# A hybrid encoder block in float32: where the second norm puts its squares, when its transposes run, and where the first values stand

## The chip, the core and the metric

The kernel runs on one core of one Trainium2 chip. Its engines work at the same time, each through its own list of instructions in order: TensorE (PE in the profile; PEld is its loading of weights), VectorE (DVE), ScalarE (ACT), GpSimd (POOL) and SyncE (SP), which here only issues loads and stores. They wait for one another by semaphores. The metric is the device time of one execution in microseconds (us), the median of several runs.

## The reference

One layer of a hybrid block on x of 1024 tokens by 1024 channels, all in float32:

```python
xn = rmsnorm(x, norm1_g[layer])
u = xn @ w_in[layer].astype(f32)
...
o_sb = stick_breaking_attention(split_heads(q_sb, SB_HEADS), split_heads(k_sb, SB_HEADS),
                                split_heads(v_sb, SB_HEADS))
...
h = x.astype(f32) + merged @ w_out[layer].astype(f32)
hn = rmsnorm(h, norm2_g[layer])
a = jnp.square(jax.nn.relu(hn @ w_ff1[layer].astype(f32)))
h = h + a @ w_ff2[layer].astype(f32)
...
return rmsnorm(h, final_g).astype(x.dtype)
```

Between the two norms lie eight heads of stick-breaking attention, four heads of a gated linear recurrence (HGRN2) and a gated merge of the two branches; the change does not touch them.

## The kernel before

**Precision.** Each float32 matrix is kept as a high and a low part: `hi_copy` (line 132, ACT) rounds to the high part, `lo_sub` (line 135, DVE) subtracts it. `three` makes a product of three matmuls, high by high, high by low and low by high. So every operand costs one ACT and one DVE instruction before PE can use it.

**Buffers.** `slot` gives one of 40 tiles of 128 by 1024, `bank` one of eight PSUM banks of 128 by 512, and the pool `wts` has two buffers each for raw, high and low weights. When a buffer is asked for and none is free, the instruction that writes it waits for the last reader of the one that is given back. Tokens are handled in eight blocks of 128 (`tb`), the first four of which are one half. Loads on SP keep their order (`load`, line 128); at most eight are open at once, so the ninth waits for the first to land.

**Order.** The text fixes the order of PE with `open_block` and `pe`; `Stream` holds jobs (projections of `w_in` and `w_out`) as generators, which `advance` and `finish` step. `after` adds an ordering edge without data. A scheduler then orders each engine's list.

**The start** (lines 150 to 200 and 1400 to 1412). SP loads x blocks 0 to 3, then six small parameter rows (`prow`), the first query/key weight (`wqk0`), x blocks 4 to 7 and the first value weight (`wv0`, two pieces). PE transposes `prow` (bank `ppar`), DVE copies it to `prm`, and a few tiny instructions make the lower bounds of the recurrence. `norm1_half` squares each block on ACT with a running sum (`token_rstd`, line 215), POOL makes the inverse root, DVE scales the block in place (line 512). `norm_transpose` transposes a half on PE, 32 transposes into eight banks `xnt`; ACT and DVE evacuate each bank into the high and low parts `xnh`, `xnl` (lines 255, 256). The first job (`first_job`) is the query/key projection of head 0: `proj_half` runs 24 matmuls of 512 columns into `pjqk` for half 0; then the second half of x is normed and transposed, 24 matmuls for half 1 follow, and then `token_steps` makes the values, 24 matmuls of 256 columns into `pjv` for each of the eight token blocks. The epilogue of `pjqk` writes `KS`, `QH`, `QL`; that of `pjv` writes `V`. After this the attention scores begin (`z`).

**The second norm** (lines 1005 to 1015 and 1476 to 1530). The last column half of `w_out` (`pw`) runs over the eight token blocks, 24 matmuls each; DVE adds each into `h` (line 1039). `norm2_token` squares the block on ACT into a slot of its own (`n_scr`), takes a further slot `hn` for the scaled block (line 1010) and stores `h` for later. `Quads` holds the transposed result in four quarters of the channels and tokens, `raw[q, kp]`. `fill(pr)` transposes two of the blocks, 16 transposes into four banks `hnt`, and ACT copies each bank in two parts into `hnq` (line 293): first quarters q 0 and q 1 of a bank, then the next bank. `plain` splits the q 0 parts of forms 1 and 2 into `sqh`, `sql`; `sums` builds the sums and differences of Strassen's scheme (line 313, `sq` and `hnq`) and `sum_form(i)` splits those into the forms 3 to 7. The first two column pairs of the up projection (`first`, class `UpPair`) then use them: `w1` multiplies form 1 and copies the bank `pW` to `p` (line 1143), `w2` adds form 2, `x6` and `x7` go to bank `pX`, `y5` to `pY`. `w1` and `w2` run in two halves of 256 columns, since columns 256 to 511 need the blocks 4 to 7. `sum_split` prepares the weights `t1h`, `t1l`, `t0h`, `t0l`.

In the driver, fills 0, 1 and 2 stand at blocks 4, 5 and 7, each after that block's `pw` matmuls and ahead of its squares; `plain` and `sums` follow them. Fill 3 comes after both pairs' `w1` and `w2` on columns 0 to 255.

Of the kernel before, what the change touches and what calls it, by code (L numbers as in the profile page):

```python
# [19 lines left out]
P = 128  # L20
# [19 lines left out]
def kernel(  # L40
# [89 lines left out]

    def hi_copy(dst, src):
        nc.scalar.copy(dst, src)  # L132

    def lo_sub(dst, src, hi):
        nc.vector.tensor_tensor(out=dst, in0=src, in1=hi.bitcast(F32), op=ALU.subtract)  # L135

    def hi_lo(h, l, src):
        hi_copy(h, src)
        lo_sub(l, src, h)
# [22 lines left out]
    for src, n in (  # L162
# [9 lines left out]

    pt = bank("ppar")
# [9 lines left out]
    nc.vector.tensor_tensor(  # L183
        out=lmx, in0=prm[:, LB0 : LB0 + 4], in1=prm[:, LB1 : LB1 + 4], op=ALU.max
    )
    for j in range(2):
        nc.vector.tensor_tensor(
            out=le[:, 4 * j : 4 * j + 4],
            in0=prm[:, LB0 + 4 * j : LB0 + 4 * j + 4],
            in1=lmx,  # L190
            op=ALU.subtract,
        )
    nc.scalar.activation(le, le, AF.Exp)
    nc.vector.tensor_tensor(out=lmx, in0=le[:, 0:4], in1=le[:, 4:8], op=ALU.add)
    nc.vector.reciprocal(lmx, lmx)
    mul(lb, le[:, 0:4], lmx)
    nc.vector.tensor_scalar(
        out=oml, in0=lb, scalar1=-1.0, scalar2=1.0, op0=ALU.mult, op1=ALU.add
    )
# [10 lines left out]
    last_evac = [None]  # L210

    def token_rstd(src, name):
        scr = slot(f"{name}_scr")
        ssq = small.tile([P, 1], F32, tag="ssq1", name=f"{name}_ss", bufs=4)
        after(nc.scalar.activation(scr, src, AF.Square, accum_out=ssq), last_evac[0])
        return inv_rms(ssq, 1, 1.0 / D, name)
# [49 lines left out]
    class Quads:  # L266
# [10 lines left out]
        def fill(self, pr, src, name):  # L277

            for kp in range(KT // 2):
# [12 lines left out]
                for q in range(2):  # L292
                    last_evac[0] = nc.scalar.copy(
                        self.part(self.raw[q, kp], pr, 1),
                        pb[:, q * 256 : (q + 1) * 256].rearrange("p (k t) -> p k t", k=2),
                    )

        def split(self, i, kp, src, pr=0, n=4):
            if (i, kp) not in self.hl:
                self.hl[i, kp] = tuple(slot(f"sq{n_}{i}{kp}", F32R) for n_ in "hl")  # L300
            h, l = (self.part(t, pr, n) for t in self.hl[i, kp])
            hi_lo(h, l, self.part(src, pr, n))

        def plain(self, i, pr, n):

            for kp in range(2):
                self.split(i, kp, self.raw[0, kp + 2 * (i - 1)], pr, n)

        def sums(self, pr, n, first=True, then=True):
            r = self.raw  # L310

            def tt(out, a, b, op):
                nc.vector.tensor_tensor(
                    out=self.part(out, pr, n),
                    in0=self.part(a, pr, n),
                    in1=self.part(b, pr, n),
                    op=op,
                )
# [189 lines left out]
    def norm1_half(half):  # L508
        for b in range(4):
            t = xt[4 * half + b]  # L510
            r = token_rstd(t, f"n1_{half}{b}")
            nc.vector.tensor_scalar(out=t, in0=t, scalar1=r, scalar2=None, op0=ALU.mult)
        yield
        yield from norm_transpose(xn, half, xt, G1, "xn", "main")
# [48 lines left out]
    def first_job():  # L563
# [3 lines left out]
        def body():  # L567
            for half in range(2):
                if half == 1:
                    u_v.split()  # L570
                    st.prefetch()
# [3 lines left out]
            yield from token_steps("pjv0", u_v, xn, range(NT), v_epilogue(0))  # L575

        return st.add([u_qk], body)
# [490 lines left out]
    class UpPair:  # L1068
# [45 lines left out]
        def sum_split(self, i):  # L1114
# [3 lines left out]
            hi_lo(h, l, self.raw[i])  # L1118
# [3 lines left out]
        def product(self, i, ps, start, stop=False, c0=0, n=512):  # L1122
            open_block("fill")
            wh, wl = self.w[i]
            for k in range(4):
# [12 lines left out]
        def w1(self, c0=0, n=512):  # L1138
# [4 lines left out]
            nc.scalar.copy(self.p1[:, c0 : c0 + n], self.W[:, c0 : c0 + n])  # L1143

        def w2(self, c0=0, n=512):
            self.product(2, self.W, False, True, c0, n)
# [333 lines left out]
    for tb in range(NT):  # L1480
# [28 lines left out]
    hn.plain(1, 3, 1)  # L1509
    hn.plain(2, 3, 1)  # L1510
# [4 lines left out]
    hn.sums(2, 2, then=False)  # L1515
# [53 lines left out]
```

## Time and profile before

| | us |
|---|---|
| median of 3 runs (1523.43 to 1525.19) | 1523.6 |
| the profiled execution | 1524.04 |
| its span, first to last instruction | 1522.3 |
| PE busy | 1488.1 |
| ACT busy | 615.4 |
| DVE busy | 961.7 |
| first `pjqk` matmul starts | 17.39 |
| first `z` matmul starts | 59.18 |
| last 16 `hnt` transposes start | 898.73 |
| first `pX` matmul starts | 910.05 |
| first `pY` matmul starts | 915.52 |
| matmuls of `x7` start | 921.72 |

A row of the timeline gives the start, the duration, the engine, the line, the operation and the tiles; in brackets stands how long the engine was idle before, and what ended that. A matmul's duration holds its way through the array; what counts for the rate is the distance between starts: 0.2275 us for 512 columns and 0.12 us for 256 at full clock. The granted clock is a share of full speed, and its mean over the execution is 0.997.

### The profile page before, as it was taken

Reading aid. Unit: us, or ns where it says so; the run is one execution under the profiler, and the core shown is the slowest. Engines: PE = TensorE matmul, PEld = TensorE weight load, DVE = VectorE, ACT = ScalarE, POOL = GpSimd, SP = SyncE. Lnnn points to the kernel's source line nnn. Section 1 sums busy time; section 2 is a strip of 40 time slices with the busy share of each in tenths; the row PEclk is TensorE's granted clock in tenths of the full one; section 3 lists DMA queues with packets and bytes.
Section 4 is the critical chain, followed back from the end, with each engine's and each line's share of the span. In section 5 each row is a group of like instructions: output and inputs, shape, how many; then the busy total and the mean of one; then the engine's idle time right before and its main releaser. Section 6 shows DMA issues by size and latency. Waiting matters only on the chain.

```text
span 1522.3 us, 19735 instructions
## 1 busy us (share of the span) xinstructions
PE 1488.1 (98%) x7677; PEld 1262.9 (83%) x7677; DVE 961.7 (63%) x1373; ACT 615.4 (40%) x1091; POOL 68.5 (5%) x242
## 2 busy tenths in 40 slices
PE   6999999999999999999999999999999999999997
PEld 5988988988898888888888888888888878888886
DVE  6589798786536554232344378766666766757765
ACT  6466576541312221222232265444444534443433
POOL 2011010000000000000000000000000000000010
PEclk9999999999999999999999999999999999999999
DMA  5223012000201001111115222344444997654744
GB/s 167 59 60 77 8 50 69 15 15 29 70 1 42 28 28 42 42 55 43 55 57 194 111 92 109 125 152 152 153 152 152 323 372 265 221 192 175 265 138 172
DMA packets 125717, 172.22 MB, mean 113 GB/s; under 512 B 22924, under 2 KB 76216, under 8 KB 125624
## 3 DMA queue, kind: packets, MB, share of 16 engines
q1 hardware_dynamic: 124088, 166.77, 32.0%
q0 software_dynamic: 1536, 4.20, 1.2%
q8 instruction: 60, 0.98, 0.3%
q14 instruction: 33, 0.27, 0.1%
HBM read 129.00 MB, written 37.75 MB: 110 GB/s over the span
## 4 chain that ended last, share of the span: by engine, by line
PE 81%; DVE 4%; issue 3%; ACT 2%; DMA 1%; POOL 1%; POOLq 0%; DVEq 0%; ACTq 0%
PE pm L121 16%; PE pjg L121 14%; PE pX L121 8%; PE py L121 6%; PE pw L121 6%; PE pY L121 6%; PE pW L121 6%; PE sl L121 3%; PE pji L121 3%; PE pjf L121 3%; PE pjq L121 2%; PE po L121 2%; PE pjv L121 1%; DVE rm L627 1%; PE z L121 1%
## 5 line engine op out<-in xcount | busy, mean ns | idle before, releaser
L132 ACT CAST whid<-w 128x1024 fp32r<-128x1024 f32 x31 | 32.7, 1054 | 165.1 <-PE pm L121 100.4
L627 DVE TENSOR_TENSOR_SCAN rm<-rm,bits 128x895 f32<-128x895 f32 (+5 forms) x64 | 86.1, 1348 | 18.8 <-ACT rm L608 17.1
L121 PE MATMUL pm<-whid,sh 128*128 128x512 f32 x248 | 96.6, 390 | 1.1 <-ACT sh L132 1.1
L121 PE MATMUL pm<-whid,sl 128*128 128x512 f32 x248 | 96.6, 389 | 0.7 <-DVE sl L135 0.7
L121 PE MATMUL pm<-wlod,sh 128*128 128x512 f32 x248 | 96.5, 389 | 0.0
L121 PE MATMUL pm<-th,sl 128*128 128x512 f32 x200 | 77.9, 390 | 0.6 <-DVE sl L135 0.6
L121 PE MATMUL pm<-th,sh 128*128 128x512 f32 x200 | 77.9, 390 | 0.0
L121 PE MATMUL pm<-tl,sh 128*128 128x512 f32 x200 | 77.9, 389 | 0.0
L135 DVE TENSOR_TENSOR sl<-sa,sh 128x1024 fp32r<-128x1024 f32 x56 | 68.2, 1218 | 2.8 <-ACT sh L132 2.8
L135 DVE TENSOR_TENSOR wlod<-w,whid 128x1024 fp32r<-128x1024 f32 x31 | 37.9, 1223 | 41.5 <-ACT whid L132 41.3
L132 ACT CAST wTh<-pw 128x128 fp32r<-128x128 f32 (+3 forms) x96 | 44.0, 483 | 45.9 <-PE pw L124 42.6
L132 ACT CAST sh<-sa 128x1024 fp32r<-128x1024 f32 x56 | 57.8, 1046 | 5.2 <-DMA sa<-ad 5.2
L121 PEld LDWEIGHTS pm<-whid,sh 128*128 128x128 f32 x248 | 46.6, 188 | 11.2 <-ACT sh L132 1.5
L121 PEld LDWEIGHTS pm<-whid,sl 128*128 128x128 f32 x248 | 46.5, 187 | 11.0 <-DVE sl L135 1.2
L135 DVE TENSOR_TENSOR wTl<-pw,wTh 128x512 fp32r<-128x512 f32 (+3 forms) x96 | 50.5, 547 | 7.7 <-ACT wTh L132 4.5
L121 PEld LDWEIGHTS pm<-wlod,sh 128*128 128x128 f32 x248 | 46.5, 188 | 9.5
L121 PEld LDWEIGHTS sl<-q,k 128*128 128x128 f32 (+1 forms) x448 | 50.2, 184 | 2.9 <-issue 1.1
L142 DVE TENSOR_TENSOR bt<-bt,rm 128x895 f32<-128x895 f32 (+5 forms) x64 | 48.2, 754 | 5.0 <-ACT bt L611 0.3
L121 PE MATMUL sl<-q,k 128*128 128x128 f32 (+1 forms) x448 | 51.3, 268 | 0.0
L945 ACT ACTIVATE g<-pjg,prm 128x512 f32<-128x512 f32 x32 | 21.9, 686 | 71.7 <-PE pjg L121 71.7
L608 ACT ACTIVATE rm<-z 128x511 f32<-128x511 f32 (+6 forms) x96 | 47.4, 500 | 7.6 <-DVE bt L142 4.5
L121 PE MATMUL pX<-sqh,t1l 128*128 128x512 f32 x128 | 49.9, 390 | 0.5 <-DVE t1l L135 0.5
(798 smaller groups left out, 4404.4 us busy)
## 6 DMA issues: line engine op xcount, KB each, us to landing
w<-in_w_ff_dram SPq DMA_DIRECT2D x72, 512.0 KB, 5.8
sa<-ad SPq DMA_DIRECT2D x56, 512.0 KB, 6.5
ad<-a SPq DMA_DIRECT2D x32, 256.0 KB, 4.3
ad<-s SPq DMA_DIRECT2D x16, 512.0 KB
x<-in_x_dram SPq DMA_DIRECT2D x8, 512.0 KB, 6.5
h<-in_x_dram SPq DMA_DIRECT2D x8, 512.0 KB, 6.7
hd<-h SPq DMA_DIRECT2D x8, 512.0 KB, 2.6
ad<-p SPq DMA_DIRECT2D x16, 256.0 KB, 3.1
```

Of the source, the lines that this page charges most:

```text
L121: return pe(nc.tensor.matmul(*a, **k))
L132: nc.scalar.copy(dst, src)
L135: nc.vector.tensor_tensor(out=dst, in0=src, in1=hi.bitcast(F32), op=ALU.subtract)
L142: nc.vector.tensor_tensor(out=out, in0=a, in1=b, op=ALU.mult)
L608: nc.scalar.activation(rm[:, s0 + c0 - 1 : s0 + m - 1], z[:, c0:m], AF.Sigmoid, scale=-0.125)
L627: nc.vector.tensor_tensor_scan(out=rr, data0=rr, data1=bits[:, 1024 - nk : 1023][:, ::-1], initial=0.0, op0=ALU.mult, op1=ALU.max,)
L945: nc.scalar.activation(dst, ps, AF.Sigmoid, bias=b)
```

## The change

It has three parts.

*Start.* SP loads x blocks 0 and 1, the six small rows, x blocks 2 and 3, `wqk0`, both pieces of `wv0`, then x blocks 4 to 7. `wqk0` is split behind the last square of half 0 and ahead of the evacuations (`hold`). The first job makes the values of a half directly behind the query/key matmuls of that half, so that four blocks of values stand between the two halves; the squares and scalings of half 1 are written ahead of them, its transposes behind them. The tiny lower-bound instructions are written later.

*Second norm.* The squares go into the tile `hn`, which the scaled block overwrites afterwards; the slot `n_scr` is gone there (the first norm keeps a slot of its own).

*Fills.* Fills 0, 1, 2 stand at blocks 4, 5, 6, behind that block's squares. A fill copies the q 0 part of a bank and splits it at once, and copies the q 1 parts of all four banks at the end; `sums` are ordered behind the last split of their fill. The first pair's `w1` on columns 0 to 255 stands ahead of block 7's squares, fill 3 stands in the middle of the second pair's `w2`, and the last `sums` cover 128 tokens instead of 256.

```diff
+    hold = [None]
+
     def hi_copy(dst, src):
-        nc.scalar.copy(dst, src)
+        after(nc.scalar.copy(dst, src), hold[0])
...
-    for tb in range(4):
-        t = slot(f"x{tb}")
-        load(t, X[tb * P : (tb + 1) * P, :])
-        xt.append(t)
+    def load_x(tb):
+        xt.append(slot(f"x{tb}"))
+        load(xt[tb], X[tb * P : (tb + 1) * P, :])
+
+    for tb in range(2):
+        load_x(tb)
...
+    for tb in (2, 3):
+        load_x(tb)
...
-    def token_rstd(src, name):
-        scr = slot(f"{name}_scr")
+    def token_rstd(src, name, scr):
         ssq = small.tile([P, 1], F32, tag="ssq1", name=f"{name}_ss", bufs=4)
-        after(nc.scalar.activation(scr, src, AF.Square, accum_out=ssq), last_evac[0])
+        last_sq[0] = after(
+            nc.scalar.activation(scr, src, AF.Square, accum_out=ssq), last_evac[0]
+        )
...
         def fill(self, pr, src, name):
...
-                for q in range(2):
-                    last_evac[0] = nc.scalar.copy(
-                        self.part(self.raw[q, kp], pr, 1),
-                        pb[:, q * 256 : (q + 1) * 256].rearrange("p (k t) -> p k t", k=2),
-                    )
+                banks.append(pb)
+                self.leave(pr, 0, kp, pb)
+                self.split(1 + kp // 2, kp % 2, self.raw[0, kp], pr, 1)
+            for kp in range(KT // 2):
+                self.leave(pr, 1, kp, banks[kp])
...
         def body():
+            v_ep = v_epilogue(0)
             for half in range(2):
-                if half == 1:
-                    u_v.split()
-                    st.prefetch()
                 ps = bank(f"{name}_{half}")
                 yield from proj_half(ps, u_qk.hl[0], xn.mov, KT, half)
                 ep(ps, half)
-            yield from token_steps("pjv0", u_v, xn, range(NT), v_epilogue(0))
+                if half == 0:
+                    u_v.split()
+                    yield
+                    st.prefetch()
+                yield from token_steps("pjv0", u_v, xn, range(4 * half, 4 * half + 4), v_ep)
...
     def norm2_token(tb):
-        r = token_rstd(hres[tb], f"n2_{tb}")
+        hsrc[tb] = slot(f"hn{tb}")
+        r = token_rstd(hres[tb], f"n2_{tb}", hsrc[tb])
         yield
-        hsrc[tb] = slot(f"hn{tb}")
...
-    for _ in norm1_half(0):
+    u_qk0, u_v0 = st.jobs[0][0]
+    norm1_half(0)
+    u_qk0.load()
+    u_v0.load()
+    for tb in range(4, NT):
+        load_x(tb)
+    hold[0] = last_sq[0]
+    u_qk0.split()
+    hold[0] = None
+    for _ in norm_transpose(xn, 0, xt, G1, "xn", "main"):
         pass
-    st.jobs[0][0][0].load()
-    for tb in range(4, NT):
-        t = slot(f"x{tb}")
-        load(t, X[tb * P : (tb + 1) * P, :])
-        xt.append(t)
-    st.advance(4, 1)
-    for _ in norm1_half(1):
+    st.advance(5, 1)
+    norm1_half(1)
+    lower_bounds()
+    st.advance(8, 1)
+    for _ in norm_transpose(xn, 1, xt, G1, "xn", "main"):
         pass
...
-        if tb in (4, 5, 7):
-            hn.fill((4, 5, 7).index(tb), hsrc, "hn")
-        if tb in (5, 6):
-            hn.plain(1, tb - 5, 1)
-            hn.plain(2, tb - 5, 1)
-        if tb == 5:
-            hn.sums(0, 1)
+        if tb == NT - 1:
+            first[0].w1(0, 256)
         side = norm2_token(tb)
         next(side)
         if tb == NT - 1:
-            hn.plain(1, 2, 1)
-            hn.plain(2, 2, 1)
-            hn.sums(1, 1)
+            hn.sums(2, 1, then=False)
+        if tb in (4, 5, 6):
+            hn.fill(tb - 4, hsrc, "hn")
+        if tb == 5:
+            hn.sums(0, 1)
         for _ in side:
             pass
+        if tb == 6:
+            hn.sums(1, 1)
     st.finish(j_wout)
     pairs[2].load()
+    first[1].w1(0, 256)
+    first[0].w2(0, 256)
     for u in first:
-        u.w1(0, 256)
-    for u in first:
-        u.sum_split(1)
-    for u in first:
-        u.w2(0, 256)
+        last_evac[0] = after(u.sum_hi(1), last_evac[0])
+    first[0].sum_lo(1)
+    first[1].w2(0, 256, range(2))
     hn.fill(3, hsrc, "hn")
-    hn.plain(1, 3, 1)
-    hn.plain(2, 3, 1)
+    first[1].w2(0, 256, range(2, 4))
     for u in first:
         u.w1(256, 256)
     for u in first:
         u.w2(256, 256)
-    hn.sums(2, 2, then=False)
+    after(first[1].sum_lo(1), hn.last_lo)
+    hn.sums(3, 1, then=False)
     hn.sum_form(6)
```

`sum_hi` and `sum_lo` are the two instructions of `sum_split` taken apart; `w2` takes the range of its four channel steps; `w1` and `sum_hi` register themselves in `last_evac`, which the next block's square is ordered behind.

More of the change, by code (lines that the diff above doesn't have):

```diff
@@ L301, in split @@
             h, l = (self.part(t, pr, n) for t in self.hl[i, kp])
[L302 to L307, printed above, removed]
+            self.last_lo = hi_lo(h, l, self.part(src, pr, n))
         def sums(self, pr, n, first=True, then=True):
@@ L312, in tt @@
             def tt(out, a, b, op):
[L313 to L317, printed above, removed]
+                after(
+                    nc.vector.tensor_tensor(
+                        out=self.part(out, pr, n),
+                        in0=self.part(a, pr, n),
+                        in1=self.part(b, pr, n),
+                        op=op,
+                    ),
+                    self.last_lo,
                 )
@@ L510, in norm1_half @@
             t = xt[4 * half + b]
-            r = token_rstd(t, f"n1_{half}{b}")
+            r = token_rstd(t, f"n1_{half}{b}", slot(f"n1scr{half}{b}"))
             nc.vector.tensor_scalar(out=t, in0=t, scalar1=r, scalar2=None, op0=ALU.mult)
-        yield
-        yield from norm_transpose(xn, half, xt, G1, "xn", "main")
     vt, qk, osb = {}, {}, {}
```

69 lines of the change are left out of this document (43 added, 26 removed).

## The prediction

> **What bounds the kernel now.** I read the page first (engine shares and the clock row), then the waits of the PE engine in the two stretches that the diff touches, then the stretches themselves by windows, then single rows of the timelines.
>
> ```profile
> PE 1488.1 (98%) x7677; PEld 1262.9 (83%) x7677; DVE 961.7 (63%) x1373; ACT 615.4 (40%) x1091; POOL 68.5 (5%) x242
> ...
> PE 81%; DVE 4%; issue 3%; ACT 2%; DMA 1%; POOL 1%; POOLq 0%; DVEq 0%; ACTq 0%
> ```
>
> The matmul engine is the bound: only 1522.3 - 1488.1 = 34.2 us of the span have no matmul. So an edit is worth what it takes from PE's idle time or from PE's slow time. The waits of PE, first from 0 to 60 us, then from 845 to 930 us:
>
> ```profile
> PE ppar L174 <- DMA prow<-in_hg_norm_g_dram: 9.5, 1, 9.5
> PE xnt L124 <- DVE x L512: 3.1, 3, 1.1
> ...
> PE pW L121 <- ACT sqh L132: 1.4, 1, 1.4
> PE pW L121 <- ACT p L1143: 0.7, 1, 0.7
> PE pW L121 <- DVE sql L135: 0.4, 1, 0.4
> ```
>
> One of the three xnt waits is in the first half's transposes; the other two (0.99 and 1.14) are in the second half's. The windows of these places (columns: length, then busy us and instructions of PE, PEld, DVE, ACT, POOL, then the granted clock, DMA share, GB/s) show a second price:
>
> ```profile
> 13.40:16.80 3.40, 3.40 (x18) 3.40 (x17) 3.16 (x5) 3.23 (x6) 0.00 (x0) 1.00 1.01 407
> 23.60:27.00 3.40, 1.54 (x12) 1.35 (x13) 1.54 (x3) 0.84 (x2) 1.27 (x2) 1.00 0.00 0
> 27.00:30.40 3.40, 3.40 (x18) 3.40 (x17) 3.40 (x6) 3.06 (x6) 0.00 (x0) 0.50 0.02 5
> 900.80:904.20 3.40, 1.74 (x12) 1.55 (x13) 3.04 (x7) 2.07 (x8) 0.00 (x0) 1.00 0.38 132
> 904.20:907.70 3.50, 3.50 (x19) 3.50 (x19) 3.50 (x6) 2.08 (x4) 0.00 (x0) 0.51 0.00 0
> ```
>
> A window that PE spends about half idle is followed by one of 3.4 us at half clock: 27.0 to 30.4 and 904.2 to 907.7. Each costs 1.7 us. Inside the slow window transposes start 0.213 us apart instead of 0.109, 256-column matmuls 0.21 instead of 0.12.
>
> Third, ACT's timeline around the second norm (start, duration, operation, idle before):
>
> ```profile
> 880.36 1.40 ACT L132 CAST sqh<-hnq 128x256 fp32r<-128x256 f32 x4
> 886.20 1.06 ACT L215 ACTIVATE n_scr<-h 128x1024 f32<-128x1024 f32 x1 [4.44 <-issue]
> ...
> 893.01 1.15 ACT L215 ACTIVATE n_scr<-h 128x1024 f32<-128x1024 f32 x1
> ```
>
> The square of token block 5 starts at 886.20, although its sum was ready at about 878.5: in the program it takes a slot that the first matmuls of block 7 (from 884.82) give back. That is the slot the new code no longer asks for.
>
> **The change, part by part.** Side by side, the two programs' instruction streams differ only from the start to the first z matmul (59.18) and from block 4 of the second wout column (870) to the first pairs' x7 (921.7); later only the slots rotate. I walk both stretches with the durations of before.
>
> *Start, the loads.* Two x tiles now go out behind six small loads. They become the ninth and tenth on SP's queue, and these wait for the first and second load to land: before, the ninth and tenth were small ones, issued at 4.54 and 5.72. So x2 goes out at 4.54 (it was about 1.6), x3 at 5.72 (about 2.1). x0 alone took 4.54 - 0.73 = 3.8 us from issue to its square; x3 by that is there at 9.5, against 8.61: +0.9 at most. The DMA view shows 410 GB/s while x2 and x3 move, 1.28 us a tile; the queue runs dry only between x1's last byte (near 5.0) and x2's first (x0's came about 1.2 us after issue, so 5.7): +0.6 to +0.7. Some of that gap holds the small loads, so +0.3 is the low end. I take +0.6: x3 normalised at 12.4, the first pjqk at 17.39 + 0.6 = 18.0. The small loads land earlier (they ended PE's wait at 9.5) but nothing follows from it, since x3 gates the transposes anyway.
>
> *Start, wqk0's split ahead of the evacuations.* ACT's cast (1.04) and DVE's subtract (1.23) run before the first evacuation instead of among them; the eight banks let PE's transposes go on. Hidden as long as wqk0 lands by about 15; before, it was cast at 14.67.
>
> *Start, values between the halves.* PE's order from 18.0: pjqk half 0, 24 at 0.2275 = 5.46; four token blocks of values, 96 at 0.12 = 11.52; 32 transposes at 0.109 = 3.5; pjqk half 1, 5.46; four more blocks, 11.52; about 0.3 at the four switches. z starts at 55.8, against 59.18: **3.4 us gained**, namely the two waits (2.1) and the slow window (1.7) with the switches, less 0.6. The cover: wv0's splits must be done by 23.5 + 1.4. ACT ends the evacuations near 18.8, the two casts (1.05 each) near 20.8, DVE the subtracts near 22.3, so about 1 us ahead of the first use. The second half of wv0 waits on SP for wqk0's subtract (14.2, to free its buffer) and x4 to x7 queue behind it: they land by about 23, their squares run after QH from 24.6, and the last is normalised near 32 (a square's start to its tile's end took 25.73 - 21.58 = 4.15). PE wants them at 35.0: 3 us of cover. Without it each us late is a us of PE. Cold start: the clock rose 4.9 us after the dense transposes began (11.86 to 16.79). If the windows lie otherwise, I reckon one to two slow lengths, 3.4 to 6.8, worth -0.8 to +0.95 us.
>
> *lower_bounds*, the hold, and the returned handles move instructions in slack of DVE and ACT at the start: nothing.
>
> *Second norm and fill.* Walk from PE's 884.82 (block 6 ends), the same as before. Block 5's square now waits for the slot that fill 1's transposes give back (879.3), so it runs near 879.6, hn5 is done at 882.9 (square to norm 2.1, norm 1.28), and fill 2 can follow block 6 at once: 16 transposes, 1.66, then block 7 to 891.9 instead of 890.25, and w1 of pair 0 to 893.4. DVE has eight 256-column sums of fill 1 (0.335 each) before block 7's addition: 893.6, not 892.1. ACT squares at 894.35 (behind p, 893.6), hn7 is done at 897.75. PE has w1, w2 and half of w2 until 896.99, so a *new wait* of 0.8. Fill 3 starts at 897.8 (898.73 before). Its splits alternate with the copies, so the first low part is there 2.2 us after the start, when the held-back six matmuls end: PE's 1.38 + 0.43 waits and the slow window go, and w1/w2 of the other columns end at 905.95 (910.05 before). From there ACT and DVE set the pace. Form 6: sums at 902.65 (six at 0.335 instead of three pairs of 1.29), cast 904.5, subtract to 906.8, PE waits 0.7 + 0.1. Form 5: a11's two squarings, two t0 casts, then sqh at 911.65, sql at 913.2 and 914.95; PE, there at 912.2, waits 0.85 + 0.4 (0.27 + 0.25 before). x7 starts at 918.95 instead of 921.72: **2.75 us gained**. The bounds: 4 if those waits are half as long, 1 if DVE's queue is another 1.7 late.
>
> The Trainium skill says otherwise of the clock: in "TensorE: Matmul & The Clock Gate" (Part 4: PE-mode transpose) transposes do not count as PE being busy, so a transpose run is idle time to the gate. The trace disagrees: the clock came up at 16.79 with only transposes issued (the first pjqk is at 17.39), and again at 30.4 after a window of nothing else.
>
> **Sum.** 3.4 + 2.75 = 6.15. The profiled execution took 1524.04 (span 1522.3 and 1.74 around it), so 1517.9; the median of the runs is 1523.6, 0.44 lower: **1517.5**. 0.2% of it is 3.05 us, about what a measurement of this kernel can tell from no change, so faster means below 1520.55.
>
> **Rivals.**
> - *The second stretch gives nothing* (0.14): hn5 misses 884.82, or DVE's queue grows, and the waits move from w1 to x6 and y5. For: DVE is busy 25.94 of the 31.44 us from 890.26 to 921.7, and four waits of my walk are on it. Against: 2 us of slack at hn5. 1523.6 - 3.4 = 1520.2.
> - *The start gives little* (0.14): x3 0.9 late and the cold clock a whole window: 3.4 - 0.3 - 0.95, and 0.2 for DVE. 1523.6 - 1.95 - 2.75 = 1518.9.
> - *The gate ignores transposes* (0.05): the 32 moved ones, 3.5 us between busy stretches, would then be a whole idle window and bring a half-clock one, 1.7: 1519.2. The skill's rule above is this; the two rises speak against it.
> - *Slower* (0.05): SP's queue. wv0's second half, held behind wqk0's subtract, and x4 to x7 behind it decide the time once wv0 lands after about 22.6 (two splits before 24.9), where I expect 18.5. Each us after that is one of PE's, and a half-idle window adds 1.7. To end 0.2% slower it must lose 9.2, by landing near 30; at 31, 1523.6 - 6.15 + 8.4 + 1.7 = 1527.6. For: all loads share this queue, and wv0's split ran only at 32.7 before. Against: that was ACT's order, not the landing.
> - *No visible change* (0.06): the gaps return later, in DVE's busy stretch 945 to 955 (9.23 of 10 us); 1523.
>
> **Chances.** My forecast 0.56. Its own range, from the bounds, is 1514.5 to 1520. Faster: 0.56, 0.12 and 0.05, and of the first rival 0.09: 0.82. Within 0.2%: 0.13. Slower 0.05. The range that leaves out 2 in 10: 1514.5 to 1521.3.
>
> **What would show it.** Right: x squares 3 and 4 start near 7.8 and 9.2; no PE wait between 18 and 55; z near 55.8; no half-clock window after the first one; block 5's square near 879.6 and 16 hnt transposes ahead of block 7; a PE wait near 1 us on hn7 and short ones on sql at pX and pY; x7 2.5 to 3 us earlier against z. Wrong: a wait of xnt on x or of pjv on wv0l; fill 2 waiting on hn5; a clock of 0.5 around 897 or 913.

## The result, and the profile after

| | us |
|---|---|
| kernel before, median of 6 runs (1522.66 to 1525.19) | 1524.28 |
| changed kernel, median of 6 runs (1516.4 to 1520.13) | 1517.84 |
| ratio, with its 95% interval | 0.996 (0.9947 to 0.9973) |
| the profiled execution, and its span | 1516.4, 1514.6 |

Of the 75 runs of the kernel before that stand beside the experiments below, one took 2501 us at a clock of 0.56 and is left out of every comparison.

The change makes the kernel faster by 0.4%. The profiled execution is 7.64 us shorter than the one before (1524.04 - 1516.4), a little more than the medians differ, 6.44; it is the fastest of its six runs. Where its span lost 7.66 us (marks on PE are starts of matmuls):

| | before | after | gained |
|---|---|---|---|
| start to first `pjqk` | 17.39 | 17.59 | -0.20 |
| first `pjqk` to first `z` | 41.79 | 37.56 | 4.23 |
| first `z` to first matmul of `x7` | 862.54 | 859.51 | 3.03 |
| `x7` to the last matmul | 591.80 | 590.74 | 1.06 |
| last matmul to the end | 8.74 | 9.20 | -0.46 |

The page of the changed kernel, engine shares and chain:

```profile
PE 1483.2 (98%) x7677; PEld 1258.7 (83%) x7677; DVE 962.1 (64%) x1379; ACT 616.2 (41%) x1091; POOL 69.1 (5%) x242
...
PE 77%; DVE 5%; issue 5%; ACT 2%; DMA 2%; POOL 1%; SPq 0%; POOLq 0%; DVEq 0%; ACTq 0%
```

PE is still the bound. Its time without a matmul went from 34.2 to 1514.6 - 1483.2 = 31.4 us, 2.8 less; the other 4.9 are busy time, which fits matmuls at full instead of half clock. The waits of PE from 0 to 60 us, then from 838 to 930 us:

```profile
PE ppar L182 <- DMA prow<-in_hg_norm_g_dram: 6.9, 1, 6.9
PE xnt L124 <- DVE x L531: 4.4, 4, 1.6
...
PE hnt L124 <- DVE hn L1029: 0.9, 1, 0.9
PE pY L121 <- DVE sql L137: 0.5, 1, 0.5
PE pX L121 <- DVE sql L137: 0.3, 1, 0.3
```

All four waits of xnt now lie ahead of the first `pjqk`; the second half of x has none. The waits of pW are gone, and in their place stand one on hn and short ones on sql, as forecast. The windows of the same places:

```profile
12.56:15.97 3.41, 2.92 (x14) 2.92 (x15) 3.28 (x7) 3.02 (x4) 0.00 (x0) 1.00 0.17 53
23.60:27.00 3.40, 3.40 (x31) 3.40 (x30) 1.38 (x2) 3.39 (x7) 1.42 (x3) 1.00 1.03 217
893.19:896.60 3.41, 2.66 (x24) 2.66 (x25) 2.59 (x4) 2.20 (x9) 0.00 (x0) 1.00 0.85 277
896.60:900.02 3.42, 3.42 (x31) 3.42 (x30) 3.30 (x8) 2.14 (x8) 0.00 (x0) 1.00 0.43 141
```

After the start, up to its last matmuls, PE is nowhere half idle for a window, and no window at half clock follows. (The column shows 1.00 in the first row too, since the record of the clock begins with its first rise, at 15.97; 14 matmuls in it instead of 31 show the half clock.) ACT's rows for the third and fourth square of x, then for block 5's in the second norm:

```profile
8.07 1.06 ACT L224 ACTIVATE n1scr<-x 128x1024 f32<-128x1024 f32 x1 [1.19 <-DMA x<-in_x_dram]
...
10.14 1.06 ACT L224 ACTIVATE n1scr<-x 128x1024 f32<-128x1024 f32 x1 [0.92 <-DMA x<-in_x_dram]
...
875.22 1.06 ACT L224 ACTIVATE hn<-h 128x1024 f32<-128x1024 f32 x1
```

The fourth square, of x block 3 (x3 from here on), is 1.5 us late against 8.61 before, not 0.6 to 0.9. Block 5's square stands at 875.22; on the clock of before (4.4 us later in this stretch) that is 879.6, the forecast's number.

### The profile page after: what moved, and what is told of

The parts are those of the page before. It is cut to its first block, busy times and chain, and to the rows that moved or that the text cites. A ratio compares the mean times of both kernels' runs of the same rounds, so it can differ in the third digit from the quotient of the medians.

```text
span 1514.6 us, 19739 instructions
## 1 busy us (share of the span) xinstructions
PE 1483.2 (98%) x7677; PEld 1258.7 (83%) x7677; DVE 962.1 (64%) x1379; ACT 616.2 (41%) x1091; POOL 69.1 (5%) x242
## 4 chain that ended last, share of the span: by engine, by line
PE 77%; DVE 5%; issue 5%; ACT 2%; DMA 2%; POOL 1%; SPq 0%; POOLq 0%; DVEq 0%; ACTq 0%
PE pm L121 15%; PE pjg L121 14%; PE pX L121 8%; PE py L121 6%; PE pY L121 5%; PE pW L121 5%; PE pw L121 4%; PE sl L121 3%; PE pjf L121 3%; PE pji L121 3%; PE pjq L121 2%; PE po L121 2%; PE pjv L121 1%; DVE rm L646 1%; PE z L121 1%
## 5 line engine op out<-in xcount | busy, mean ns | idle before, releaser
L137 DVE TENSOR_TENSOR sl<-sa,sh 128x1024 fp32r<-128x1024 f32 x56 | 68.3, 1220 | 2.0 <-ACT sh L134 2.0
```

Source lines behind the costliest of these rows:

```text
L137: return nc.vector.tensor_tensor(out=dst, in0=src, in1=hi.bitcast(F32), op=ALU.subtract)
```

## The experiments

Every run is compared with runs of the kernel before on the same chip. The table has the marks of all profiles; "half clock" gives the starts of the 3.41 us windows at half clock after the first rise. The three rows named after are the same kernel.

| profile | first `pjqk` | first `z` | `z` to `x7` | half clock | ratio (95%) |
|---|---|---|---|---|---|
| before | 17.39 | 59.18 | 862.54 | 27.0, 904.3 | |
| after | 17.59 | 55.15 | 859.51 | none | 0.9960 (0.9947 to 0.9973) |
| after_again | 19.53 | 57.09 | 859.86 | none | 0.9965 (0.9953 to 0.9977) |
| after_third | 18.06 | 55.61 | 859.92 | 1225.0 | 0.9967 (0.9955 to 0.9978) |
| start_only | 18.59 | 56.14 | 861.20 | 1225.7 | 0.9990 (0.9981 to 0.9999) |
| norm2_only | 16.72 | 59.00 | 859.78 | 25.9, 1227.4 | 0.9986 (0.9977 to 0.9995) |
| squares_only | 16.90 | 59.15 | 862.51 | 25.9, 903.1, 1230.8 | 0.9999 (0.9990 to 1.0008) |
| kept_busy | 16.52 | 57.86 | 861.34 | none | 0.9991 (0.9982 to 1.0001) |
| late_splits | 18.79 | 56.38 | 861.17 | none | 0.9970 (0.9960 to 0.9981) |
| h7_first | 18.87 | 56.46 | 860.16 | 1226.5 | 0.9975 (0.9966 to 0.9984) |
| loads_x_first | 17.40 | 54.97 | 859.75 | none | 0.9959 (0.9946 to 0.9972) |
| loads_first_again | 16.52 | 54.06 | 859.83 | none | 0.9948 (0.9934 to 0.9962) |
| warm | 16.50 | 54.23 | 860.02 | none | 0.9944 (0.9931 to 0.9956) |
| warm_lb_late | 15.42 | 53.15 | 860.14 | none | 0.9947 (0.9933 to 0.9962) |

### Each half of the change alone

start_only is the new kernel with the old functions `fill`, `sums`, `norm2_token` and the old driver from the second norm to form 6; norm2_only is the new kernel with the old first job, `norm1_half`, loads and driver of the start. The core of the two, against the new kernel, first start_only, then norm2_only:

```diff
-        hsrc[tb] = slot(f"hn{tb}")
-        r = token_rstd(hres[tb], f"n2_{tb}", hsrc[tb])
+        r = token_rstd(hres[tb], f"n2_{tb}", slot(f"n2_{tb}_scr"))
         yield
+        hsrc[tb] = slot(f"hn{tb}")
...
-        if tb in (4, 5, 6):
-            hn.fill(tb - 4, hsrc, "hn")
+        if tb in (4, 5, 7):
+            hn.fill((4, 5, 7).index(tb), hsrc, "hn")
```

```diff
-    for tb in (2, 3):
-        load_x(tb)
...
-                yield from token_steps("pjv0", u_v, xn, range(4 * half, 4 * half + 4), v_ep)
+            yield from token_steps("pjv0", u_v, xn, range(NT), v_epilogue(0))
```

> The start of the new kernel (loads, early weight split, first values between the halves) with the second norm and the fills of the old one. Theory of the prediction, with the sizes that the trace of the changed kernel shows: z starts near 55.2 (59.18 before), everything from the second norm on is as before, so the median lies 4.0 us below the kernel before, ratio 0.9974. Rival (the two parts are not separate: the start alone changes what the later stretch waits for): a ratio of 0.9985 or more, or 0.9965 or less. Rival (the gain of the start is a clock accident of one execution): z again near 57 or later and a ratio of 0.9985 to 1.0.

> The start of the old kernel with the second norm, the fills and the pairs' order of the new one. Theory of the prediction: 2.6 to 2.75 us between the last output projection and the first x7, no half-clock window there, PE waits of about 0.9 on hn and 0.3 to 0.6 on sql at pX and pY; the median lies 2.6 us below the kernel before, ratio 0.9983. If the 0.6 to 0.8 us that the trace of the changed kernel also gained far behind x7 (near 1220 and 1495) come from this part, 3.4 us and 0.9978. Rival (second stretch gives nothing, the waits only move): ratio above 0.9993.

In the profiles each half does what it did in the whole: `z` 3.04 us earlier with the new start, `x7` 2.76 us nearer to `z` with the new fills. The medians say less, 1.5 and 2.1 us, and their sum of 3.6 is below the 5.0 to 6.1 that the three measurements of both halves together give. The second half's interval (0.8 to 3.5 us) holds the profile's size; the first half's (0.15 to 2.9 us) ends just short of 3.04. By the marks set for start_only, its ratio of 0.9990 is the rivals' figure and not the theory's 0.9974, while `z`, at 56.14, lies between the two. So the medians do not show the sizes of the halves; that the two act apart is read from the profiles alone. One possible reason is to be seen in start_only's profile. Its windows at the old fills, then at the first products of the down projection:

```profile
898.02:901.43 3.41, 2.02 (x14) 1.82 (x15) 3.32 (x8) 1.83 (x8) 0.00 (x0) 1.00 0.30 103
901.43:904.85 3.42, 3.42 (x31) 3.42 (x30) 3.42 (x6) 2.62 (x5) 0.00 (x0) 1.00 0.02 5
1222.29:1225.70 3.41, 1.58 (x7) 0.68 (x6) 2.55 (x3) 3.41 (x4) 0.00 (x0) 1.00 1.02 396
1225.70:1229.12 3.42, 3.42 (x9) 2.65 (x10) 3.42 (x4) 0.26 (x1) 0.00 (x0) 0.50 1.04 397
```

The old fills' waits are all there (1.4, 0.7 and 0.4 us, as before), yet no half-clock window follows: the boundaries lie otherwise against the work, and the window that holds the waits is busy for 2.02 us instead of 1.8. With that, `z` to `x7` is 861.20 instead of 862.54. At 1222 it is the other way round: a wait that every version has, 0.6 to 1.5 us long in the profile's count, was followed by a half-clock window here and not in the profile of before. So whether a given wait costs its length alone, or over a microsecond more, changes from execution to execution. Sums of single profiles hide this; medians hold some of it. The runs without a profile show the same. By these numbers a half-clock window takes 0.0011 off the mean granted clock of an execution (3.41 × 0.5 of about 1520 us). The half clock behind the last matmul, 3.5 to 6.7 us long in the 14 profiles, takes another 0.0012 to 0.0022 and delays no matmul. So a run at 0.999 has had no such window, as the profile of the changed kernel, and one at 0.995 two or more. Of the other 74 runs of the kernel before, 13 have 0.999 and take 1520.4 to 1521.4 us, and 19 have 0.995 and take 1524.0 to 1526.2.

### PE kept busy in the old waits

```diff
+                    if half == 1 and kt == 0 and b >= 2:
+                        for _ in range((9, 11)[b - 2]):
+                            transpose(pb[:, b * P : (b + 1) * P], ident)
                     transpose(
...
+    open_block("fill")
+    for _ in range(11):
+        transpose(first[0].W[:, 256:384], ident)
     for u in first:
         u.w1(256, 256)
```

> The kernel before with 31 transposes of the identity added where PE waits: 9 and 11 ahead of the third and fourth transposes of the second half of x, 11 ahead of the first pair's form 1 on columns 256 to 511. They write places that are overwritten afterwards, and last less than the waits (1.0 of 1.16, 1.2 of 1.36, 1.2 of 1.43 us), so no work starts earlier by them at an equal clock. Theory A (a window that PE spends half idle brings a half-clock one, and transposes count as work): no window of 0.5 near 27 nor near 904, z 1.7 us earlier than 59.18, x7 3.4 us earlier in an execution that would have had both; the median falls by 1.7 to 2.5 us, since both profiles with the old start had the first slow window but only one of two with the old fills the second: ratio 0.9984 to 0.9989. Theory B (transposes do not count as work for the gate): the slow windows stay, ratio 0.9998 to 1.0005. Theory C (the slow windows have another cause than idle time): the same as B.

Both half-clock windows are gone. The windows of the two places:

```profile
23.60:27.00 3.40, 3.24 (x29) 2.83 (x28) 1.54 (x3) 0.83 (x2) 1.27 (x2) 1.00 0.02 5
27.00:30.40 3.40, 3.40 (x27) 3.15 (x25) 3.40 (x6) 3.40 (x7) 0.00 (x0) 1.00 0.00 0
899.06:902.47 3.41, 2.80 (x23) 2.36 (x22) 2.50 (x6) 2.62 (x10) 0.00 (x0) 1.00 0.45 144
902.47:905.90 3.43, 3.43 (x31) 3.43 (x30) 3.43 (x7) 1.83 (x4) 0.00 (x0) 1.00 0.00 0
```

`z` comes 1.25 us before the mean of the other three old starts (59.11), and `x7` 1.2 us nearer to `z`, without any work starting on earlier data. So idle time brings the half clock, and transposes count as work: theory A in its mechanism. Its twelve runs have a mean clock of 0.9981 against 0.9963 in the 24 of the kernel before beside them, so not only the profile shows it. In size it fell short: 1.4 us in the median, with an interval that just touches no change, where 1.7 to 2.5 were expected. At the fills a half-clock window costs less than 1.7 us: 256-column matmuls start 0.213 us apart in it instead of 0.12, which makes 1.5 of 3.41 us, and the first wait at pY behind it is 0.10 us after a half-clock window and 0.23 without one.

### The squares alone

```diff
-        r = token_rstd(hres[tb], f"n2_{tb}")
+        hsrc[tb] = slot(f"hn{tb}")
+        r = token_rstd(hres[tb], f"n2_{tb}", hsrc[tb])
         yield
-        hsrc[tb] = slot(f"hn{tb}")
```

> The kernel before with one part of the change: the squares of the second norm go into the tile of the scaled block. Theory A (the prediction: it only makes room, since fill 2 still stands behind block 7's matmuls): block 5's square starts near 879.6 instead of 886.20, block 5 is scaled near 883, PE's order and its waits of 1.4, 0.7 and 0.4 stay, ratio 0.9995 to 1.0005. Theory B (the late square also delays block 7's scaling through DVE's queue: at 888.36 and 890.42 two scalings stand ahead of block 7's addition at 891.62): the addition starts 1.3 us earlier, block 7's scaling with it, the waits behind fill 3 shrink by up to 0.7, ratio 0.9993 or less.

The time does not change, but both theories were wrong about the square of block 5. ACT's timeline of squares_only:

```profile
886.11 1.06 ACT L216 ACTIVATE hn<-h 128x1024 f32<-128x1024 f32 x1 [4.44 <-issue]
```

It is as late as ever (886.20 before). In the program the tile `hn` of block 5 now asks for the slot that `n_scr` had asked for, and still waits for the same first matmuls of block 7: in both profiles it starts 0.09 us after the fifth of them ends (886.11 in before, 886.02 here). In the new kernel the same instruction starts 0.3 us after the last transposes of fill 1 end (874.91). One slot less is asked for in both; the earlier square comes with the new order of the fills. Which slot is given is read from these times and the program, not from the trace itself, and the new order without the freed slot was not tried.

### The splits of fill 3 behind its copies

```diff
                 self.leave(pr, 0, kp, pb)
-                self.split(1 + kp // 2, kp % 2, self.raw[0, kp], pr, 1)
+                if pr < 3:
+                    self.split(1 + kp // 2, kp % 2, self.raw[0, kp], pr, 1)
             for kp in range(KT // 2):
                 self.leave(pr, 1, kp, banks[kp])
+            if pr == 3:
+                hold[0] = last_evac[0]
+                for kp in range(KT // 2):
+                    self.split(1 + kp // 2, kp % 2, self.raw[0, kp], pr, 1)
+                hold[0] = None
```

> The new kernel, but in fill 3 alone the four casts of the low quarter stand behind all eight copies, as they did before. Theory A (the prediction: alternating is what ends PE's waits behind fill 3): the first cast at 897.5 instead of 895.12, its low part near 899, PE waits 1.2 to 2 us behind the six held-back matmuls; some half of it is found again at pX and pY, where the waits of 0.47, 0.62 and 0.25 shrink: 0.7 to 1.5 us slower than the new kernel, and one more place where a slow window can follow. Theory B (DVE's queue decides until x7 anyway): the waits at pX and pY shrink by all of it, x7 within 0.3 us of the new kernel's distance from z (859.5), the same time.

PE's waits in this stretch of late_splits:

```profile
PE pW L121 <- ACT sqh L134: 1.1, 1, 1.1
PE hnt L124 <- DVE hn L1035: 0.9, 1, 0.9
PE pY L121 <- DVE sql L137: 0.5, 1, 0.5
```

The old wait on sqh is back, `z` to `x7` is 1.3 to 1.7 us longer, and 0.3 is found again at pX, where the wait fell from 0.47 to 0.19 (counted, as in the forecast, as the distance between two starts less the usual pace; the profile's idle time is about 0.17 us less for the same wait). That is theory A: DVE's later queue does not swallow a PE wait at this point. The median, 0.9970 against 0.9960 to 0.9967, lies on the same side, with intervals that overlap.

### Block 7's addition ahead of the sums

`behind` holds block 7's addition into `h` for the eight sums of fill 1, then block 7's scaling for the six of fill 2.

```diff
-        if tb == 6:
-            hn.sums(1, 1)
...
         if tb == NT - 1:
-            hn.sums(2, 1, then=False)
+            hn.sums(1, 1)
...
+    behind[0] = hn7[0]
+    hn.sums(2, 1, then=False)
...
-                    self.last_lo,
+                after(after(ins, self.last_lo), behind[0])
```

> The new kernel with DVE's order changed: the eight sums of fill 1's quarters stand behind block 7's addition instead of ahead of it, and the six of fill 2 behind block 7's scaling. Theory A (the new PE wait on hn comes from block 7's addition queueing behind sums): the addition starts near 888 instead of 889.18, hn7 is done 1.2 us earlier, PE's wait of 0.94 before fill 3 goes, and x7 starts 0.9 us earlier: near 1516.9. Theory B (DVE is the bound up to x7, so an earlier fill 3 only moves the wait): the hn wait goes, the waits on sql at pX and pY grow by as much, x7 within 0.3 us of 914.66, time 1517.8. Theory C: the sums now come too late for form 6, and the time is 0.5 to 1 us longer.

PE's waits in the same stretch of h7_first:

```profile
PE pW L121 <- DVE sql L137: 0.9, 1, 0.9
PE pY L121 <- DVE sql L137: 0.5, 1, 0.5
PE hnt L124 <- DVE hn L1028: 0.2, 1, 0.2
```

The wait on hn falls from 0.9 to 0.2, and one of 0.9 on sql comes up at pW, because the six sums and a weight's subtract now stand ahead of fill 3's subtracts on DVE. `z` to `x7` is 860.16, 0.2 to 0.65 longer than in the new kernel, and the ratio is higher (0.9975 against 0.9960 to 0.9967), with intervals that overlap. That is theory B's mechanism, an earlier fill 3 only moves the wait, though the wait comes up at pW and not at pX and pY, and at a price; theory C's 0.5 to 1 us is not ruled out. An order with the six sums behind fill 3's subtracts was not tried.

### The order of the first loads

```diff
-    for tb in range(2):
+    for tb in range(4):
         load_x(tb)
...
-    for tb in (2, 3):
-        load_x(tb)
```

> The new kernel with one thing undone: x blocks 2 and 3 are loaded ahead of the six small rows again, so that they are no longer the ninth and tenth on the queue. Theory A (the late x3 costs PE time): x3's square starts at 8.6 instead of 10.14, the dense transposes 1.4 us earlier, the first pjqk 0.7 to 1.4 us before 17.59 as the clock comes up, and the time is 0.7 to 1.4 us below the new kernel: near 1516.8. Theory B (what follows the transposes decides: the small rows now end PE's wait only at 9.5, and the weights come later): pjqk within 0.3 us of 17.59 and the time that of the new kernel, 1517.8. Theory C (the clock comes up a window later when the transposes begin earlier): up to 1 us slower, 1518.8.

> The new kernel once more, beside the same runs of the kernel before as the next three. Theory A (the two parts add up as in the traces, 4.0 and 2.6 us): ratio 0.9957. Theory B (the two single parts, 0.999 and 0.9986, are right and the first measurement of the new kernel was low): ratio near 0.9976. Theory C (what the profile shows of half-clock windows is a draw of each execution, since the windows begin at another time against the work in each of the six profiles so far: at 16.79, 15.97, 17.38, 15.66, 17.02 and 18.14 us modulo 3.41): the ratio lies between, 0.9963 to 0.9972, and the profile shows slow windows that the first one did not, such as one near 1222, where PE waits 1.6 to 2.5 us for the first weights of the down projection.

loads_x_first alone did not decide. x3's square came at 8.58 and the dense transposes 1.4 us earlier, as theory A has it, but the clock rose only at 17.02, and `pjqk` at 17.40 is within theory B's 0.3 us of the first profile; the median, 1517.02, is nearer to A.

after_again came out between: ratio 0.9965, theory C's range, though its interval holds A's and B's figures too, and with the latest `z` of all new starts. Its windows at the start show why:

```profile
9.20:12.62 3.42, 0.95 (x2) 0.37 (x2) 0.93 (x3) 1.25 (x4) 1.42 (x4) 1.00 1.01 250
12.62:16.03 3.41, 2.51 (x12) 2.51 (x13) 3.25 (x7) 2.71 (x4) 0.06 (x1) 1.00 0.16 53
16.03:19.44 3.41, 3.41 (x18) 3.41 (x17) 3.10 (x5) 2.74 (x5) 0.00 (x0) 1.00 0.91 297
```

The dense transposes begin at 13.52, inside a window that ends up 73% busy; that does not raise the clock, so a whole further window passes at half clock, up to 19.44. In the first profile they began at 13.05, the window was 86% busy, and the clock rose at 15.97. The 29 transposes took 6.25 and 4.79 us. The half-clock window near 1222 that the expectation named did not come in this profile; it came in after_third.

> The new kernel with the old order of the first loads, once more: the five runs of it so far have a median of 1517.02, the eleven of the new kernel 1517.93. Theory A (x3 comes 1.5 to 2 us late in the new order because the weights are issued 0.4 us behind it and share the engines; in each profile the first pjqk then stands at 17.59 to 19.53, mean 18.7, against 16.7 to 17.4 with the old order): z near 54.5 to 55.5, median 1 to 1.5 us below the new kernel, 1516.5 to 1517.5. Theory B (no cost: the clock's draw made the difference): z spread as before, median 1518 to 1518.5.

With the old order of the loads the first `pjqk` stands at 17.40 and 16.52, against a mean of 18.57 in the six profiles with the new one. `z` is at 54.97 and 54.06, against a mean of 56.14. The ratios point the same way, 0.9959 and 0.9948 against 0.9960, 0.9965 and 0.9967, but their intervals overlap. By the profiles the new load order costs about 1.6 us of what the rest of the change gains. What all loads moved in the first 20 us, in slices of 0.5 us, in before and then in after:

```profile
GB/s 0 0 0 123 156 328 262 393 401 451 401 377 377 426 404 131 32 151 271 106 133 212 172 303 353 318 377 401 401 410 401 434 428 371 375 346 260 234 233 305
GB/s 0 0 0 49 229 336 377 451 410 264 92 205 360 352 139 205 279 350 279 254 287 244 206 268 338 264 96 2 0 0 0 41 186 344 371 426 442 361 287 352
```

In before the four x blocks move in one piece up to 7.5. In the new order there is a gap near 5.0, between x1 and x2, and a second one from 7.0 to 8.0, between x2 and x3. From 8.5 on the first weights, issued from 6.12, move beside x3: of the 367 packets that start between 8.5 and 9.5, 309 are below 512 bytes, where those of x have 4096. How much of x3's delay is the gap and how much the shared queue was not tested apart.

### The clock raised before the data comes

```diff
+    for _ in range(36):
+        transpose(pt[:, 128:256], ident)
     pe(nc.tensor.transpose(pt[:, :NPR], prow, ident[:NPR, :NPR]))
...
+                    if half == 0 and kt == 0 and b == 3:
+                        for _ in range(9):
+                            transpose(pb[:, b * P : (b + 1) * P], ident)
```

> The new kernel with x blocks 2 and 3 ahead of the small rows again, and 45 transposes of the identity added in PE's idle time at the start: 36 ahead of the parameters' transpose (7.7 us at half clock, between 2.3, when the identity is written, and 9.4, when the rows land; less if the clock comes up meanwhile) and 9 ahead of the first one that waits for x3. They write places that are overwritten or not read. Theory A (the half clock of the first 15 to 19 us costs PE time, and whether it ends at 15.6 or 19.4 is a draw of each execution): the clock is full before the dense transposes begin at 11.6, 29 of them take 3.2 us instead of 4.5 to 6; then ACT's and DVE's evacuations (eight at 0.67, the first low part near 15.5) pace the first query/key matmuls, which start at 15.4 to 15.8 instead of 17.4 and end near 20.9; wv0's low part may cost 0.4. z at 53.0 to 53.6, where the five profiles with the new loads show 55.15 to 57.09 and loads_x_first 54.97; the median is 1.5 us below loads_x_first and the runs lie closer together: 1515.5. Theory B (the evacuations bind already, PE's clock is hidden there): z within 0.4 us of 54.97, time 1517.0. Theory C (transposes do not raise the clock): the first full clock at 15.6 to 19.4 as in the others.

The second version also puts the lower bounds behind the last evacuation of the first half on DVE:

```diff
-    lower_bounds()
+    lower_bounds(xn_low[0])
```

> The kernel of run warm (old order of the first loads, 45 added transposes at the start) with the tiny lower-bound instructions ordered behind the evacuations on DVE. In warm they stood between the subtract of the first weight and the evacuations, 15.02 to 15.79, because their exponential had got behind the weight's cast on ACT, and PE waited 1.2 us for the first low part. Theory A (the evacuations on DVE pace the start once the clock is full): the first evacuation at 15.1 instead of 15.70, the first pjqk near 15.9 instead of 16.50, z near 53.6 instead of 54.23; median 0.6 us below warm, 1515.5 to 1516.2 where the kernel before takes 1523.8. Theory B (the landing of the first weight at 12.7 sets it, and the rest is the same chain): the same z as warm and loads_first_again, 54.1 to 54.3.

> The new kernel beside the run above, for a comparison on one chip at one time. Theory A (the new order of the first loads costs 1 to 2 us, and the clock's draw spreads z from 55.2 to 57.1): ratio near 0.9965 as before, 1.5 to 2.5 us above the run above. Theory B (the orders of the loads are equal): within 0.7 us of it.

In warm the clock was full from 5.08 and the last of the transposes began at 15.05, yet `pjqk` began only at 16.50: PE waited 1.2 us for the first low part, behind the weight's split and the tiny instructions. So theory A is right on the clock, but most of the gain was hidden, and `z`, at 54.23, lies between its range and theory B's. With the tiny instructions out of the way, in warm_lb_late, the start on PE reads:

```profile
2.24 5.64 PE L124 MATMUL ppar<-ident 128*128 128x128 f32 x36 [2.24 <-POOL ident masks.py:199]
10.21 0.23 PE L181 MATMUL ppar<-ident,prow 44*128 44x44 f32 x1 [2.32 <-DMA prow<-in_hg_norm_g_dram]
...
11.88 3.38 PE L124 MATMUL xnt<-ident,x 128*128 128x128 f32 x29
15.42 0.50 PE L121 MATMUL pjqk<-xnh,wqk0h 128*128 128x512 f32 x1
```

`pjqk` and `z`, at 15.42 and 53.15, are the earliest of all, 0.5 us ahead of theory A's figures. Beside it on the same chip the new kernel had 1519.38 (9 runs, 1517.65 to 1521.15) and this one 1516.07 (5 runs, 1514.8 to 1517.98): 0.2% below the new kernel and 0.53% below the kernel before. The two differ by 3.3 us, more than the 1.5 to 2.5 expected. To judge by loads_first_again, most of that is the load order; what the early clock and the moved instructions add to it is seen in the profile (`z` 0.9 and 1.8 us earlier than in the two with the load order alone), but the medians of these four versions (0.9944 to 0.9959) do not tell them apart.

## Why the prediction was right

The forecast of 1517.5 met 1517.84 and its mechanism was in the main the one that acted. That it was met within 0.4 us is partly luck: against 6.15 us of gain forecast, the ratio of this measurement gives 6.1, those of the two later ones of the same kernel 5.3 and 5.0. Term by term (waits counted as distances between starts, as in the forecast):

- *Start, 3.4 us.* Measured 4.03 in the first profile, and 2.97 as a mean over six profiles of the new start (56.14) and three of the old (59.11). Two sizes inside were off and partly cancelled. "x3 by that is there at 9.5", which gave the first `pjqk` at 18.0: its square came at 10.14 to 11.08 in the six profiles with the new loads, and `pjqk` at 18.57 in the mean against 17.00 for the old start, 1.6 late and not 0.6. The bound was taken from x0's issue to its square, 3.8 us; x3 took 4.4 to 5.3 in the six profiles. The step that failed is "the queue runs dry only between x1's last byte (near 5.0) and x2's first": it runs low a second time, from 7.0 to 8.0, and then x3 shares it with the first weights, as shown with the order of the first loads. The other way, from `pjqk` to `z` the new order takes 37.57 instead of 42.11, 4.5 us less, where the forecast's own numbers make it 4.0.
- *"No pjv or x wait between the halves."* Right, with less cover than reckoned: wv0's low part was done at 22.50 and needed at 23.25; the last x block was scaled at 32.88 and needed at 34.65 (1.8 us, not 3).
- *Second norm and fills, 2.75 us.* 2.6 to 3.0 against the profile of before. The walk holds step by step: block 5's square at the forecast's place, fill 2 directly behind block 6 (880.43), a wait of 0.94 before fill 3 (0.8 forecast; the scaling of block 7 ended 0.5 us late), 0.47 at pX (0.8) and 0.62 + 0.25 at pY (0.85 + 0.4).
- *"That is the slot the new code no longer asks for."* Not so by itself, as squares_only shows; the late square goes with the new order of the fills, the freed slot included.
- *The half-clock windows, 1.7 us each, taken as certain.* This is a matter of chance and not a fixed price. At the x waits all three profiles that keep them idle have it; at the old fills two of three, and there it is worth 1.3 us (862.5 against 861.2 and 861.3 of `z` to `x7`), not 1.7. Without it the second part is worth about 1.5 us (861.3 less a mean of 859.8). The runs at a mean clock of 0.999 show what the change is worth without any such window: the 13 of the kernel before have a median of 1520.76, the seven of the new one (in its three measurements) 1517.65, 3.1 us less. So, as far as these few runs tell, about half of the gain of 5 to 6 us is half-clock windows that no longer come.
- *The gate and transposes.* The rival by the Trainium skill's rule ("TensorE: Matmul & The Clock Gate", Part 4: PE-mode transpose), that transposes don't count as PE being busy, fell: with nothing but transposes issued the clock rose at 5.08 in warm, and kept_busy held it up with them. That these are the page's transpose mode is taken from the program's `nc.tensor.transpose`; the trace calls them MATMUL.

The remaining gain of the first profile, 1.06 us behind `x7`, has nothing to do with the change as far as the other profiles show: over half of it is the wait near 1220 for the down projection's first operands, 1.28 in before and 0.72 in after, and 0.8 to 1.6 in the others, whichever half of the change they hold. What stays open in part is why the two halves measured alone add up to 3.6 us in the medians; their intervals are too wide to call it a loss. The kernel before beside them had a mean clock of 0.9971, and 0.9963 and 0.9966 beside the two later measurements of the whole. At the 1 us or so per 0.001 that its runs show (1520.76 at 0.999, 1524.98 at 0.995), this takes an estimated 0.5 to 0.8 us off each half.

## What to carry to other kernels

A wait on the bound engine has two prices, its length and a half-clock window that may follow; the second depends on where the clock's windows fall in that execution, so take it with a chance, not as a sum. Moving ready work between two dependent phases was worth more here (4.5 us) than hastening either, and the cheap-looking part of such an edit, two loads moved behind small ones, gave a third of it back (`pjqk` 1.6 us later). Where several instructions ask for buffers from one ring, test the freed buffer together with the order that uses it.

## What the runs showed of the hardware

*When the clock falls and rises.* In 14 profiles the changes lie on a grid of 3.41 us whose place against the kernel differs each time (first full clock between 5.08 and 19.44). The Trainium skill says so in "TensorE: Matmul & The Clock Gate", Part 1: The HAM clock gate (the "warmup" mystery): the window runs freely and does not start with the kernel; these traces agree. The traces also show how busy a window must be: ten full-clock windows ahead of the last matmuls in which PE was busy 30 to 53% of the time were followed by half clock, none at 55% or more. The share does not decide alone. One window at 48% in warm, and those of 46, 47 and 53% in which the last matmuls end in loads_first_again, after and start_only, were not followed by half clock; in these four PE's work is one unbroken piece, in the ten it lies in two to four. Why that matters is open. From the cold state windows of up to 73% left the clock down, and one of 80% raised it. So 1.6 us of idle time within one window, in several pieces, was enough to lose the clock (before, 900.84 to 904.26, 53% busy).

*POOL beside DVE.* Half a microsecond on the way to the wait before fill 3 is POOL's. Its first instruction of an inverse root takes 0.19 us (876.46, DVE idle) and took 0.73 while DVE ran sums:

```profile
891.20 0.73 POOL L213 TENSOR_SCALAR n_ss<-n_ss 128x1 f32<-128x1 f32 x1 [6.27 <-DVE hnq L330]
892.01 0.55 POOL L216 TENSOR_TENSOR n_y<-n_ss,expo 128x1 f32<-128x1 f32 x1
```

It ends as DVE's last sum ends (891.88). In before the same instruction took 1.21 (888.47) beside a scaling of 1.28 on DVE (888.36), and ended with it too. The Trainium skill, "SBUF — State Buffer", Who interferes with whom, says that a DVE instruction with two SBUF inputs contends with a GpSimd one that reads SBUF; the trace agrees, with 0.54 us for one such meeting; no run here takes the two apart.
